# Moving work between queues and engines in the S5 stage of a two-layer hybrid trunk

## The chip, the cores and the metric

The kernel runs on one core of one Trainium2 chip. The metric is the device time of one execution in microseconds (us); lower is better. Engines are named as the profile names them: PE (TensorE matmul), PEld (TensorE weight load), DVE (VectorE), ACT (ScalarE), POOL (GpSimd) and SP (SyncE, which only issues transfers). Each of them works through its own program in order.

## The reference

One inference step of a trunk with two layers, for 1024 prompt tokens and 32 sample tokens that share all weights. Layer 0 mixes tokens by retention and forgetting attention, layer 1 by an S5 state-space layer with a gated linear unit. Each mixer is followed by cross-attention to 256 memory tokens and a squared-ReLU MLP. All of it is float32 with a model width of 1024. The change lies in the S5 mixer alone:

```
u = (h @ w_in_c).reshape(B, T, 64 groups, 16 channels)
bu = einsum(b_bar, u)                  # per group: 64 complex states
x_t = a * x_{t-1} + bu_t               # diagonal complex recurrence (associative scan over t)
y = Re(einsum(c, x)) + d * u
g = y @ w_glu;  out = g[..., :1024] * sigmoid(g[..., 1024:])
outputs also: the last state of the prompt and of the sample (real, imaginary)
```

## The kernel before, in words

Activations lie feature-major (features on partitions, tokens along the free axis) in three token groups of 384, 384 and 256 + 32. Each large product runs as three passes over exact splits x = hi + lo and w = hi + lo. A weight block is loaded by `wload` (L135, SP queue, two buffers `wst`), split by ACT (`wh`, L139) and DVE (`wl`, L140), and used by 72 matmuls.

The S5 layer works on chunks of 8 tokens, 132 chunks in all (128 of the prompt, 4 of the sample), in eight blocks f of 8 groups (128 features). For each block:

- `gemm` with `winc` gives u block by block; `evac_u` (L1438, DVE) moves each token group from PSUM to the tile `u`, scaled by the reciprocal rms.
- `s5_block` stores `u` to DRAM (`ud`, L1445) and loads it again in eight pieces (L1448) as the tile `U`, with one token of the chunk and one channel to a partition, so that one product contracts a whole chunk. `u` has two buffers and `U` three. It also loads the tables `Gm` (L1450) and `ET` (L1453); `Hm` (L1422) and `Tm` (L1424) of the next block are loaded after `outputs`.
- `states` multiplies `Gm` with `U` (PE), ACT copies the result into `VC` (L1467, L1468), and a rotation by the phase table `ET` turns the complex recurrence into a real one: p1 = VC * cos (L1471) and p2 = VC * sin (L1472), a sum and a difference (L1473, L1474), a scan for each part with the radii `RT` (L1479), and a second rotation back (L1482, L1483). Four instructions (L1488, L1489, twice each) put the states into `Xp`. Three small copies (L1491 to L1493) save the last states in `so` and put the sample's first state `x0s` into a column of `Xp`. `s5_radii` (L1429) fills `RT` for the next block.
- `outputs` multiplies `Tm` with `U` and `Hm` with `Xp`, ACT copies to `yt` (L1504), and the ACT queue stores it to `yd` (L1505).

After the eight blocks come the memory keys and values of layer 1 (`memory_k` and `memory_v`: `mt`, `wxk`, `wxv`), between whose products the last blocks' `states` and `outputs` are placed, then the loads of `yd` as `yf` (L1533), their splits (L1524, L1525) and the product with `wglu`.

The program of PE is written down in order. The object `po` counts the columns of the products laid out so far; `states` of a block is due S1 = 16.5 such microseconds after its `u` is complete and at least 12 after the `states` before it, `outputs` S2 = 20 after `states`. The programs of the other engines, and of the queues that they issue, are put in order by the framework's scheduler from priorities and its own model of time.

Of the kernel before, what the change touches and what calls it, by code (L numbers as in the profile page):

```python
"""Hybrid retention / forgetting-attention / S5 streaming step on one core.

Activations are feature-major: features on partitions, tokens along the free axis; the 1024 prompt
tokens and the 32 sample tokens share every weight (token groups of 384, 384 and 256 + 32).
Large float32 products run as three float32r passes over exact splits x = hi + lo, w = hi + lo
(hi*hi + hi*lo + lo*hi); small products run in float32.
"""
# [11 lines left out]
AF = mybir.ActivationFunctionType  # L19
# [12 lines left out]
class _Order:  # L32
    """The tensor engine's program is laid out piece by piece; a piece that waits for other engines
    is put off until enough other products stand before it."""
# [29 lines left out]
def _body(tc, A):  # L64
    nc = tc.nc
# [20 lines left out]
    with es:  # L86
# [17 lines left out]
        # ---------------- constants  # L104
# [22 lines left out]
        # ---------------- helpers  # L127
# [20 lines left out]
        # evacuations can be held back until the pool they write to may be opened  # L148
# [14 lines left out]
        def gemm(blocks, load, rhs, evac, gran, done=None, post=None, lead=0, final=(0, 1, 2)):  # L163
            """blocks of 128 outputs, gran at a time for each token group; the first `lead` advance together"""
            blocks = list(blocks)
            at = 0
            while at < len(blocks):
                n = gran(at) if callable(gran) else gran
                bl = blocks[at : at + n]
                at += n  # L170
                ws = [load(b) for b in bl]
                for g in final if at >= len(blocks) else range(3):
                    i = 0
                    while i < len(bl):
                        w = lead if lead else 1
                        lead = 0
                        pss = [bank()[:, : NG[g]] for _ in range(w)]
                        for k in range(8):
                            s = slice(k * 128, k * 128 + 128)
                            x = rhs(g, k)  # L180
                            for j in range(w):
                                wh, wl = ws[i + j]
                                mm3(pss[j], wh[:, s], wl[:, s], x[0], x[1], k == 0, k == 7)
                            po.tick()
                        for j in range(w):
                            def ev(b=bl[i + j], g=g, ps=pss[j]):
                                with tc.high_priority(offset=HP):
                                    evac(b, g, ps)
                                if post is not None:
                                    post(b, g)  # L190
                            submit(ev)
                        i += w
                    if done is not None and at >= len(blocks):
                        submit(lambda g=g: done(g), False)
# [9 lines left out]
        def rstd_cols(acc, nt, scale, half=False, r=None, tag="rc", ps=None):  # L204
            """acc: [128, nt*128] partial sums of squares by partition -> [128, nt] reciprocal rms.
            With r, the columns summed up still lack a factor r^2."""
            ps = bc() if ps is None else ps
            for t in range(nt):
                mm(ps[:, t : t + 1], acc[:, t * 128 : t * 128 + 128], ones_c, start=True, stop=True)
            ms = npl.tile([128, 4], F32, tag="ms", bufs=4, name="ms")  # L210
            if r is None:
                nc.vector.tensor_scalar(ms[:, :nt], ps[:, :nt], scale, EPS, op0=MULT, op1=ADD)
            else:
                r2 = npl.tile([128, 4], F32, tag="r2", bufs=3, name="r2")
                gtt(r2[:, :nt], r[:, :nt], r[:, :nt], op=MULT)
                stt(ms[:, :nt], ps[:, :nt], scale, r2[:, :nt], op0=MULT, op1=MULT)
                vtt(ms[:, :nt], ms[:, :nt], r2[:, :nt], op=MULT)
                nc.vector.tensor_scalar(ms[:, :nt], ms[:, :nt], EPS, None, op0=ADD)
            rc = npl.tile([128, 4], F32, tag=tag, bufs=4 if tag == "rc" else 6, name=tag)
            tails.append(gtt(rc[:, :nt], ms[:, :nt], mhalf[:, :nt], op=ALU.pow))  # L220
            if r is not None:
                gtt(rc[:, :nt], rc[:, :nt], r2[:, :nt], op=MULT)
            if half:
                nc.vector.tensor_scalar(rc[:, :nt], rc[:, :nt], 0.5, None, op0=MULT)
            return rc
# [21 lines left out]
        def update(o, g, ys, acc, gpost, xres, xout, last=False, row=False, scale=1.0 / 1024, half=False, r=None):  # L247
            """x + rmsnorm(y) * g; o gets the split of the new x times the next norm's gain, and its
            reciprocal rms by token, in columns or along a row of all partitions"""
# [71 lines left out]
        # ---------------- memory keys and values of a layer (prompt)  # L321
# [63 lines left out]
        # ---------------- state-space layer: discretisation and per-group chunk matrices  # L385
# [8 lines left out]
        def s5_prepare(sp):  # L394
# [10 lines left out]
            # angles lambda_im*dt * (1, 8, 16, ..., 512), reduced to [-pi, pi]  # L405
# [20 lines left out]
            # powers a^0..a^8  # L426
# [19 lines left out]
            # input gains  # L446
# [26 lines left out]
            def group(f):  # L473
# [20 lines left out]
                def cmul(xr, xi, pr, pi, n, nm, neg):  # L494
                    """outer products over (power, channel): real part and (negated) imaginary part"""
# [20 lines left out]
                # phase table e^{i n theta}, n = 1..128 and again 1..4  # L516
# [45 lines left out]
        # the tensor engine runs in the order written down  # L562
        es.enter_context(tc.manual_schedule(engines={mybir.EngineType.PE}))

        # ---------------- layer 0: input
# [41 lines left out]
        with tc.tile_pool(name="m0", bufs=1, reuse_waits="tile") as m0, tc.tile_pool(name="s5p", bufs=1, reuse_waits="tile") as s5p:  # L607
            # values and gates of the forgetting attention
# [43 lines left out]
            # log forget gates and their running sums  # L652
# [52 lines left out]
            # queries and keys of the forgetting attention  # L705
# [10 lines left out]
        # ---------------- layer 0: retention  # L716
# [29 lines left out]
        def chain(h, qT, kT, sil, step):  # L746
            """Chunks of queries/keys against themselves and the state before them, one after the other."""
# [23 lines left out]
            def values(t, p, kw, qs):  # L771
# [16 lines left out]
                # group norm over the head, back to feature-major, gate  # L788
# [56 lines left out]
        # ---------------- layer 0: forgetting attention  # L845
# [7 lines left out]
        with tc.tile_pool(name="m2", bufs=1, reuse_waits="tile") as m2:  # L853
            # causal masks, added to the scores by a product with the identity
# [7 lines left out]
            for s in range(2):  # L862
# [5 lines left out]
                # values beside ones: the last row of the product is the sum of the weights  # L868
# [22 lines left out]
            def fox_max(hd):  # L891
                """row maxima of the scores, negated, as two more rows of the query side; in pieces"""
# [32 lines left out]
            def fox_out(hd, more):  # L925
                """transposed scores, weights, values; more: the pieces of the next head's maxima"""
# [19 lines left out]
                def weigh(lo, hi, ri):  # L946
                    """the products over the sums, split"""
# [71 lines left out]
        # sample queries against the cache and themselves  # L1019
# [86 lines left out]
        def proj_out(nblk, load, rhs, evac_y, gpost, xres, xout, gran=4, lead=0, **kw):  # L1106
            """the product with the output weights, its norm and the residual; returns what becomes of it by group"""
# [35 lines left out]
        def close_after(stack, out, gs, then):  # L1143
            """before the first evacuation into it opens the next pool, where what comes before leaves off"""
# [7 lines left out]
        def cross(l, X, left, right):  # L1152
            """attention to the memory; returns its output and the pools to close behind it"""
# [11 lines left out]
            def parts(hd, name):  # L1165
                """two halves of an operand: of even heads in the pool, of odd heads in idle tiles of the norms"""
# [42 lines left out]
            def attend(hd, g):  # L1209
                """pieces of the attention of a head for a group of tokens, spread over the products that follow"""  # L1210
# [161 lines left out]
        def cross_mlp(l, X, p, last, left, right):  # L1372
            """returns the new x by group and the pools still in use"""
# [25 lines left out]
        # ---------------- layer 1: state-space mixer  # L1399
# [27 lines left out]
        def s5_radii(f):  # L1427
            RT = sd["RT"] = sd["sp"].tile([128, 4, 132], F32, tag="RT", bufs=1, name="RT")
            nc.vector.tensor_copy(RT, r8[:, 4 * f : 4 * f + 4][:, :, None].to_broadcast([128, 4, 132]))  # L1429
# [11 lines left out]
        def s5_block(f, u):  # L1441
# [3 lines left out]
            dma(Ud[f][:, :, :], u)  # L1445
            U = sd["su"].tile([128, 8, 132], F32, tag="U", bufs=3, name="U")
            for j in range(8):
                dma(U[16 * j : 16 * j + 16], Ud[f][:, j, :].rearrange("(g c) n -> c g n", c=16))  # L1448
# [6 lines left out]
            def states():  # L1455
                """chunk inputs to the states, and the states by a scan over the chunks"""
# [15 lines left out]
                gtt(p2, VC, sinb, op=MULT)  # L1472
# [10 lines left out]
                gtt(p2, p1, sinb, op=MULT)  # L1483
# [7 lines left out]
                nc.vector.tensor_copy(so[:, 8 * f : 8 * f + 8, 0], xg[:, :, 128])  # L1491
                nc.vector.tensor_copy(so[:, 8 * f : 8 * f + 8, 1], xg[:, :, 132])
                nc.vector.tensor_copy(xg[:, :, 128], x0s[:, 8 * f : 8 * f + 8])  # L1493
# [53 lines left out]
        gate = {}  # L1547
# [16 lines left out]
# ---------------------------------------------------------------- host side: layout only  # L1564
# [129 lines left out]
```

## Time and profile before

| | before |
|---|---|
| median of 3 runs | 3298.36 us (3295.52 to 3303.45) |
| span of the profiled execution | 3296.3 us |
| PE busy | 3160.3 us (96%) |
| DVE busy | 1495.2 us (45%) |
| ACT busy | 1071.6 us (33%) |
| POOL busy | 914.5 us (28%) |
| mean granted TensorE clock | 0.980 |

The only time that goes with the profiled execution is its span from the first to the last instruction, 3296.3 us. The median of the three runs is 2.1 us longer, and their lowest is 0.8 us shorter than that span. A busy share is a mean over stages with different limits; the stage that the change touches lies between about 1850 and 2056 us of the span. The granted clock is given as a share of 2.4 GHz, so that 0.50 is 1.2 GHz. Where an idle time is given with a releaser, that is the event that came last before the instruction began.

### The profile page before, as it was taken

How to read it: one execution, taken by the hardware profiler on the slowest of the kernel's cores; microseconds unless marked ns; L12 is line 12 of the kernel's file. 1: busy time of each engine (PE TensorE's matmuls, PEld its weight loads, DVE VectorE, ACT ScalarE, POOL GpSimd, SP SyncE). 2: the span in 40 equal slices, each digit the busy share in tenths (PEclk: the TensorE clock that was granted, in tenths of full speed). 3: DMA queues.
4: the chain of work that ended last, by engine and by line, in shares of the span. 5: the costliest groups of instructions: out<-in, count | busy, mean ns of one | idle time of the engine just before them, and what ended most of it. 6: DMA issues, size and time to landing. Idle time of an engine off the chain costs nothing.

```text
span 3296.3 us, 50246 instructions
## 1 busy us (share of the span) xinstructions
PE 3160.3 (96%) x19972; PEld 3059.2 (93%) x19972; DVE 1495.2 (45%) x2756; ACT 1071.6 (33%) x2117; POOL 914.5 (28%) x1182
## 2 busy tenths in 40 slices
PE   7999999998999999999999888998999999999997
PEld 7899986688999999999999878998999999999997
DVE  8843566527435223332334797227426132233224
ACT  5212335425435322221124334225435321222212
POOL 4873431216115211111114442015106111111115
PEclk9999999999999999999999998999999999999998
DMA  5562244124114211110112677114124110111113
GB/s 157 156 194 70 62 137 128 38 58 141 52 42 128 65 42 52 52 47 31 52 52 74 204 241 222 57 52 141 49 66 124 52 47 32 52 52 52 39 58 99
DMA packets 176336, 285.71 MB, mean 87 GB/s; under 512 B 34027, under 2 KB 130508, under 8 KB 175972
## 3 DMA queue, kind: packets, MB, share of 16 engines
q1 hardware_dynamic: 132310, 215.02, 21.8%
q10 hardware_dynamic: 35328, 41.83, 3.8%
q0 software_dynamic: 8464, 25.66, 2.3%
q8 instruction: 157, 2.57, 0.3%
q14 instruction: 77, 0.63, 0.1%
HBM read 220.17 MB, written 66.39 MB: 87 GB/s over the span
## 4 chain that ended last, share of the span: by engine, by line
PE 77%; DVE 7%; POOL 6%; DMA 4%; issue 4%; ACT 2%; SPq 0%; DVEq 0%; ACTq 0%; POOLq 0%
PE mm L72 68%; PE a L72 4%; PE b L72 2%; POOL q L527 2%; POOL acc L245 2%; PE c L72 1%; DVE xl L202 1%; DVE wl L140 1%; DVE upd L274 1%; POOL ET L528 1%; DMA ed<-ET 1%; POOL ET L529 1%; DVE upd L273 1%; PE b L76 1%; DMA mt<-in_memt_dram 0%
## 5 line engine op out<-in xcount | busy, mean ns | idle before, releaser
L72 PE MATMUL mm<-xh,wh 128*128 128x384 f32 (+1 forms) x3168 | 1050.4, 332 | 6.5 <-ACT mo L382 3.7
L72 PE MATMUL mm<-xh,wl 128*128 128x384 f32 (+1 forms) x3168 | 1031.4, 326 | 7.4 <-DVE wl L140 7.3
L72 PE MATMUL mm<-xl,wh 128*128 128x384 f32 (+1 forms) x3168 | 1031.9, 326 | 1.2 <-DVE xl L202 1.2
L72 PE MATMUL mm<-ho,wh 128*128 128x384 f32 (+1 forms) x3456 | 822.9, 324 | 1.5 <-DVE y L1366 1.5
L72 PEld LDWEIGHTS mm<-xh,wh 128*128 128x128 f32 x3168 | 603.5, 190 | 13.8 <-issue 5.0
L72 PEld LDWEIGHTS mm<-xh,wl 128*128 128x128 f32 x3168 | 602.4, 190 | 9.0 <-DVE wl L140 9.0
L72 PEld LDWEIGHTS mm<-xl,wh 128*128 128x128 f32 x3168 | 603.5, 190 | 1.8 <-DVE xl L202 1.8
L72 PEld LDWEIGHTS mm<-ho,wh 128*128 128x128 f32 x3456 | 603.5, 188 | 1.8 <-DVE y L1366 1.8
L72 PE MATMUL mm<-ho,wl 128*128 128x384 f32 (+1 forms) x1728 | 558.2, 323 | 0.0
L1347 POOL TENSOR_TENSOR ho<-u,ho 128x384 fp32r<-128x384 f32 (+1 forms) x192 | 183.3, 955 | 1176.2 <-ACT ho L1346 1150.4
L140 DVE TENSOR_TENSOR wl<-wst,wh 128x1024 fp32r<-128x1024 f32 (+1 forms) x252 | 318.5, 1264 | 416.0 <-ACT wh L139 412.8
L139 ACT ACTIVATE wh<-wst 128x1024 fp32r<-128x1024 f32 (+1 forms) x252 | 266.5, 1059 | 708.9 <-PE mm L72 641.6
L245 POOL TENSOR_TENSOR acc<-acc,sq 128x384 f32<-128x384 f32 (+2 forms) x259 | 280.9, 1093 | 412.1 <-ACT sq L244 406.5
L1366 DVE TENSOR_TENSOR y<-y,mm 128x384 f32<-128x384 f32 (+1 forms) x336 | 174.3, 519 | 353.4 <-PE mm L72 353.2
L72 PEld LDWEIGHTS mm<-ho,wl 128*128 128x128 f32 x1728 | 325.5, 188 | 0.0
L1344 DVE TENSOR_TENSOR u<-u 128x384 f32<-128x384 f32 (+1 forms) x192 | 103.3, 538 | 409.7 <-ACT u L1343 409.7
L1343 ACT ACTIVATE u<-mm 128x384 f32<-128x384 f32 (+1 forms) x192 | 88.0, 458 | 313.8 <-PE mm L72 313.6
L1346 ACT ACTIVATE ho<-u 128x384 fp32r<-128x384 f32 (+1 forms) x192 | 95.7, 498 | 172.1 <-DVE u L1344 172.1
L1206 POOL TENSOR_SCALAR p<-p,mx 128x256 f32<-128x256 f32 (+1 forms) x72 | 36.7, 510 | 241.4 <-DVE mx L1205 138.8
L202 DVE SCALAR_TENSOR_TENSOR xl<-upd,gall,xh 128x384 fp32r<-128x384 f32 (+1 forms) x120 | 100.0, 834 | 5.1 <-ACT xh L201 4.8
L244 ACT ACTIVATE sq<-y 128x384 f32<-128x384 f32 (+1 forms) x126 | 61.9, 495 | 109.7 <-DVE y L1366 56.2
L72 PE MATMUL mm<-xo,wh 128*128 128x384 f32 (+1 forms) x384 | 92.1, 324 | 0.0
(427 smaller groups left out, 4132.9 us busy)
## 6 DMA issues: line engine op xcount, KB each, us to landing
wst<-in_wup_dram SPq DMA_DIRECT2D x64, 512.0 KB
wst<-in_wdn_dram SPq DMA_DIRECT2D x64, 512.0 KB
xs<-upd ACTq DMA_DIRECT2D x80, 192.0 KB
xr<-xs SPq DMA_DIRECT2D x80, 192.0 KB
wst<-in_wab_dram SPq DMA_DIRECT2D x20, 512.0 KB
wst<-in_wxk_dram SPq DMA_DIRECT2D x16, 512.0 KB
wst<-in_wxv_dram SPq DMA_DIRECT2D x16, 512.0 KB
wst<-in_wxq_dram SPq DMA_DIRECT2D x16, 512.0 KB
```

The costliest lines, as they stand in the source:

```text
L72: return nc.tensor.matmul(out, lhsT, rhs, **kw)
L139: act(wh[:, :n], st[:, :n], AF.Copy)
L140: vtt(wl[:, :n], st[:, :n], wh[:, :n].bitcast(F32), op=SUB)
L202: stt(l, src, gain, h.bitcast(F32), op0=MULT, op1=SUB)
L244: act(sq[:, :n], src, AF.Square)
L245: return gtt(acc[:, :n], acc[:, :n], sq[:, :n], op=ADD)
L527: gtt(o[:, :, :, :m], ET[:, :, :, :m], a_, op=MULT)
L1343: act(t, ps, AF.Relu)
L1344: vtt(t, t, t, op=MULT)
L1346: act(h, t, AF.Copy)
L1347: gtt(lo, t, h.bitcast(F32), op=SUB)
L1366: vtt(Y[g][o], Y[g][o], ps, op=ADD)
```

## The change

Within the S5 stage, (1) the store of `u` and the eight loads of `U` of each block are issued by POOL and no longer by SP; (2) the product with the sines in both rotations is computed by DVE and no longer by POOL, so that DVE computes both products of both rotations; (3) the three small copies at the end of `states` and the copy that fills the radii are done by ACT and no longer by DVE. Line numbers stay as they are; comments and docstrings were removed as well.

```
 def s5_radii(f):
-    nc.vector.tensor_copy(RT, r8[:, 4 * f : 4 * f + 4][:, :, None].to_broadcast([128, 4, 132]))
+    act(RT, r8[:, 4 * f : 4 * f + 4][:, :, None].to_broadcast([128, 4, 132]), AF.Copy)
 ...
 def s5_block(f, u):
-    dma(Ud[f][:, :, :], u)
+    nc.gpsimd.dma_start(Ud[f][:, :, :], u)
     U = sd["su"].tile([128, 8, 132], F32, tag="U", bufs=3, name="U")
     for j in range(8):
-        dma(U[16 * j : 16 * j + 16], Ud[f][:, j, :].rearrange("(g c) n -> c g n", c=16))
+        nc.gpsimd.dma_start(U[16 * j : 16 * j + 16], Ud[f][:, j, :].rearrange("(g c) n -> c g n", c=16))
 ...
     def states():
         vtt(p1, VC, cosb, op=MULT)
-        gtt(p2, VC, sinb, op=MULT)
+        vtt(p2, VC, sinb, op=MULT)
 ...
         vtt(VC, p1, cosb, op=MULT)
-        gtt(p2, p1, sinb, op=MULT)
+        vtt(p2, p1, sinb, op=MULT)
 ...
-        nc.vector.tensor_copy(so[:, 8 * f : 8 * f + 8, 0], xg[:, :, 128])
-        nc.vector.tensor_copy(so[:, 8 * f : 8 * f + 8, 1], xg[:, :, 132])
-        nc.vector.tensor_copy(xg[:, :, 128], x0s[:, 8 * f : 8 * f + 8])
+        act(so[:, 8 * f : 8 * f + 8, 0], xg[:, :, 128], AF.Copy)
+        act(so[:, 8 * f : 8 * f + 8, 1], xg[:, :, 132], AF.Copy)
+        act(xg[:, :, 128], x0s[:, 8 * f : 8 * f + 8], AF.Copy)
```

## Rows read from the trace of the kernel before

**Rows 1.** Stretches: length, busy time by engine, granted clock, DMA share, GB/s.
```profile
1910.00:1980.00 70.00, 54.22 (x372) 52.90 (x372) 68.61 (x93) 26.66 (x61) 29.25 (x29) 0.95 0.77 253
1980.00:2000.00 20.00, 18.56 (x147) 18.39 (x147) 16.66 (x26) 3.62 (x7) 6.20 (x8) 0.92 0.73 220
2000.00:2056.00 56.00, 47.27 (x351) 45.21 (x350) 39.38 (x43) 32.66 (x51) 15.82 (x17) 0.90 0.72 226
```

**Rows 2.** Waits of PE, 1800 to 2060: releaser, total us, times, longest.
```profile
PE b L72 <- DMA Tm<-td: 7.1, 3, 2.9
PE mm L72 <- DVE u L1438: 5.7, 2, 4.4
PE a L72 <- DMA yd<-yt: 4.3, 1, 4.3
...
```

**Rows 3.** Timeline of POOL, block 4: start, duration, instruction, idle before.
```profile
1939.31 2.41 POOL L1472 TENSOR_TENSOR p<-VC,ET 128x1056 f32<-128x1056 f32 x1 [1.01 <-ACT xmh L201]
...
1947.88 2.64 POOL L1483 TENSOR_TENSOR p<-p,ET 128x1056 f32<-128x1056 f32 x1 [6.16 <-DVE ini L1476]
```

**Rows 4.** Timeline of DVE beside them, and one row of the tail.
```profile
1939.41 2.34 DVE L1493 COPY Xp<-x0s 128x8 f32<-128x8 f32 x1
1941.66 1.24 DVE L1471 TENSOR_TENSOR p<-VC,ET 128x1056 f32<-128x1056 f32 x1
...
1948.11 3.52 DVE L1482 TENSOR_TENSOR VC<-p,ET 128x1056 f32<-128x1056 f32 x1
...
2004.83 3.49 DVE L140 TENSOR_TENSOR wl<-wst,wh 128x1024 fp32r<-128x1024 f32 x1
```

**Rows 5.** Groups by line, shapes apart: count, busy us, mean ns, idle before.
```profile
L140 DVE TENSOR_TENSOR wl<-wst,wh 128x1024 fp32r<-128x1024 f32 x248 | 312.8, 1262 | 415.1 <-ACT wh L139 411.9 <-PE mm L72 3.0
L976 ACT ACTIVATE pT<-b 128x512 f32<-128x512 f32 x48 | 28.4, 593 | 32.3 <-PE b L72 32.2
L1472 POOL TENSOR_TENSOR p<-VC,ET 128x1056 f32<-128x1056 f32 x8 | 21.6, 2700 | 12.2 <-issue 6.8 <-ACT VC L1468 4.0 <-ACT xmh L201 1.4
L1482 DVE TENSOR_TENSOR VC<-p,ET 128x1056 f32<-128x1056 f32 x8 | 19.0, 2374 | 0.0
L1493 DVE COPY Xp<-x0s 128x8 f32<-128x8 f32 x8 | 11.5, 1432 | 0.0
L1471 DVE TENSOR_TENSOR p<-VC,ET 128x1056 f32<-128x1056 f32 x8 | 10.0, 1249 | 4.0 <-ACT VC L1468 4.0
```

**Rows 6.** Two lines' instructions: ns min/median/max, first and last start.
```profile
L1491 DVE COPY so<-Xp x8: 163/172/1966, 1889.1 to 2022.2; 128x8 f32<-128x8 f32 x8
...
L1429 DVE COPY RT<-r x8: 435/1303/2637, 1847.1 to 1984.9; 128x528 f32<-128x528 f32 x8
```

**Rows 7.** Transfers issued: ns min/median/max, first and last start; then landing of L1533 on POOL.
```profile
L1448 SPq DMA_DIRECT2D U<-ud x64: 303/429/1655, 1860.8 to 1986.1; - x64
L1424 POOL DMA_DIRECT2D Tm<-td x8: 530/530/602, 1847.7 to 2007.2; - x8
L1533 POOL DMA_DIRECT2D yf<-yd x4: 590/612/642, 2044.2 to 2046.0; - x4
DMA to landing us min/median/max: 4.8/5.1/5.2
```

**Rows 8.** Timeline of SP and PE around block 6's loads.
```profile
1952.32 0.34 SPq L1445 DMA_DIRECT2D ud<-u  x1
...
1965.37 0.30 SPq L1448 DMA_DIRECT2D U<-ud  x1
...
1968.74 0.69 PE L72 MATMUL a<-U,Gm 128*128 128x132 f32 x4 [4.28 <-DMA yd<-yt]
```

**Rows 9.** Timeline of POOL and PE around two table loads.
```profile
1846.87 0.81 POOL L1422 DMA_DIRECT2D Hm<-hd  x1
...
1936.68 0.53 POOL L1424 DMA_DIRECT2D Tm<-td  x1
...
1941.61 0.46 PE L72 MATMUL b<-U,Tm 128*128 128x132 f32 x2 [2.84 <-DMA Tm<-td]
```

## The prediction

> **What bounds the kernel now.** The page first: PE is busy for 96% of the span, so over the whole kernel only idle PE time, or a better granted clock, can be won. Then the table of stretches shows where such time lies in the stage that the change touches [rows 1]. Between 1910 and 1980 us PE works for 54.22 of 70 us and idles for 15.8, while DVE is busy for 68.61: there DVE is the bound, though over the span it is busy for only 45%. From 1980 to 2000 PE idles for 1.4 us, from 2000 to 2056 for 8.7. The granted clock is 0.95, 0.92 and 0.90 in these stretches; one minus the clock, times the busy time, is 2.7, 1.5 and 4.7 us, an estimate of what the lower level (1.2 GHz instead of 2.4) cost. Idle time and clock together are 34.8 us, about 1% of the time; no change in this stage can win more in it.
>
> Then the waits of PE [rows 2]. Three of them have to do with the change: `Tm` comes late three times (7.1 us), the copy of `u` out of PSUM comes late on DVE (5.7 us), and one wait of 4.3 us stands in front of the product of `Gm` and `U`. That last one is put down to the store of `yt`, but the timeline says otherwise: `u` of block 6 was stored at 1952.32, the last piece of `U` was issued at 1965.37, and the product began at 1968.74 [rows 8]. I read it as a wait for `U`. `Tm` is late because POOL issues it late: in block 4 it was issued at 1936.68 and PE began at 1941.61, 4.9 us later [rows 9], and POOL's program has the rotation's second product ahead of it, as at 1947.88 [rows 3].
>
> Last, the two timelines side by side. POOL's product runs from 1939.31 for 2.41 us; DVE's copy of eight columns into `Xp` (L1493) starts at 1939.41 and lasts 2.34 us, and the cosine product begins only then [rows 3, 4]. In the second rotation POOL works from 1947.88 for 2.64 us, and DVE's product L1482 lasts 3.52 us from 1948.11. The same shape alone takes 1.25 us (L1471), and the small copies next to L1493 take 0.17 (median) [rows 5, 6]. So DVE stands still for most of the time in which POOL computes: giving the product to POOL does not take it off DVE.
>
> The Trainium skill says so too (SBUF — State Buffer, section "SBUF: two separate sides"): DVE and GpSimd share one pair of ports as an exclusive lock held for a whole instruction. The trace agrees: 3.52 us against 1.25.
>
> **The change, part by part.**
>
> **The products (POOL to DVE).** Added to DVE: two products a block of the shape of L1471, 2 x 1.25 = 2.50 us. Removed from DVE a block, by means and medians [rows 5, 6]: `RT` 1.30, the column of `x0s` 1.43, the two `so` copies about 0.5 (median 0.17 each, one of them 1.97), and the stretch of L1482, 2.37 - 1.25 = 1.12. That is 4.35 us, net -1.85. Within the saturated stretch the pattern of rows 4 is commoner than the mean: 2.34 for the column, 2.27 of stretch, 0.34 for `so`, and an `RT` of 0.44, its shortest; 5.39 in all, net -2.9. I take -2.4 us a block between these two. Four blocks pass in the 70 us (a block every 17 us or so), so DVE's work there shrinks by 10 us (7 to 12). It stays the bound or nearly: PE has 54.2 us of work against the 58.6 left to DVE. So the 10 us come out of PE's idle 15.8, and the waits for `u` and most of those for `Tm` with them.
>
> **The clock.** If 10 of 15.8 us of idle time go, part of the 2.7 + 1.5 us lost at the lower clock comes back; I take 2 (0 to 4.2).
>
> **The tail, 2000 to 2056.** Block 7's rotations lie between the weight splits there. One `wl` took 3.49 us instead of 1.26 while POOL computed [rows 4, 5]; that and block 7's own 1.9 would give 4.1 us of DVE. But PE waits there mostly for weights that pass through two `wst` buffers one after the other, so I count 2 us (0 to 4.1).
>
> **The copies and radii (DVE to ACT).** ACT gets four instructions a block. `RT` is 528 columns; the nearest ACT row has 512 and takes 0.59 us. The copies of eight columns lie between DVE's 0.16 and that 0.59. So 1.1 to 2.4 us a block, on an engine that is busy for 26.66 of 70 us [rows 1, 5, 6]: the work itself is covered by ACT's idle time. The price is the order: `RT` waits for the scan, the copies for `Xp`, and behind them on ACT stand the evacuations of `VC` and `yt`, which free PSUM for PE, and the weight splits `wh`. The path from `Xp` to PE's `outputs` hardly changes: three short ACT copies replace 0.34 + 1.43 us on DVE. I take +1 us in all; from 0 to +1 a block, 8 in all.
>
> **The loads and stores of u (SP to POOL).** POOL loses 16 products, 8 x (2.41 + 2.64) = 40 us by the two durations in rows 3, and gets 64 pieces and 8 stores. The piece most like them is `yf` as POOL issues it, 0.61 us; a store is like `Tm`, 0.53 [rows 7]. So 39 + 4 = 43 us: its busy time stays. Eight pieces take 4.9 us instead of 8 x 0.43 = 3.4 on SP, so `U` is complete 1.5 us later where nothing else holds it. The chain is store 0.53, landing 5.1, pieces 4.9, landing 5.1: 15.6 us, taking the `yf` landing for both. `states` is due 16.5 us of products after `u` is complete, so this just fits; before, block 6 needed 1968.74 - 1952.32 = 16.4. In front of the waiting store and pieces on POOL stand `Gm`, `ET`, and behind them `Tm`, `Hm` and the small memset of `Xp`; PE waits for all of these. I take +1 us; from -4.3 (the wait before block 6's product goes, since `U` no longer stands behind other loads on SP) to +1.5 a block, 12 in all. SP loses 72 issues, and weight loads no longer stand behind stores that wait for `u`; PE hardly waits for weights in the saturated stretch, so I count nothing (at best the 2 us of the tail once more).
>
> A rule of the skill speaks against this part: while DVE runs an instruction that uses both ports, such as a float32 copy, GpSimd can't write its descriptors, and a transfer issued from its queue stalls (SBUF — State Buffer, the box on DVE blocking DMA in "SBUF: two separate sides"; it gives 620 ns becoming about 3100). One row bears it out weakly: `Hm` took 0.81 us to issue, `Tm` 0.53 in the median and at most 0.60, mostly with DVE saturated beside it [rows 7, 9]. It is part of the second rival.
>
> **Sum.** -10 (DVE) - 2 (clock) - 2 (tail) + 1 (ACT) + 1 (POOL) = -12. The profiled span of 3296.3 becomes 3284.3. The median of the runs is 2.1 us above that span, which I keep: 3286.4, given as 3286.
>
> **The rivals.**
>
> *All of PE's gaps close.* If DVE falls below PE in every block and SP, free of waits for `u`, runs weights and `U` ahead, then 15.8 + 1.4 + about 4 us of idle time and 6 of the 8.9 us of clock come back: 27 us, 3271. For it: DVE's 58.6 is near PE's 54.2. Against it: PE needs `U`, `Tm` and the rotations in turn, and the tail is paced by its loads. Chance 0.15.
>
> *POOL becomes the late one, and the kernel slower.* Place: POOL's program between two `outputs`. If a block's store and pieces are put ahead of the next `Tm`, then `Tm` is issued 0.53 + 5.1 + 4.9 = 10.5 us after its buffer comes free, or later if `u` is not ready, and lands 4.9 later: 15.4 us. PE has some 13.5 us until it needs it (54.2 / 4 for all its work in a block), less some 3 that `outputs` itself takes (16 products, an estimate from four of that width in 0.69 us [rows 8]): about 10.5. So PE would wait 5 us in each of six blocks, 30 us, where it now waits 18 in all; with the clock's share this is about 10 us over before, 3308. It decides from about 7 us between the release of `Tm` and its issue; at 5 it costs what it costs today. Issues stretched as the one `Hm` was (0.28 us x 72 = 20 us) push the same way. For it: POOL works in order, and a store that waits for `u` holds all behind it. Against it: `Tm` is issued at high priority, and it becomes ready with the pieces, not after them. Chance 0.20.
>
> *Nothing moves.* The transfers are the bound behind DVE: the DMA share is 0.77 in the saturated stretch and 0.72 in the tail [rows 1], and the same bytes must pass; the relief of DVE turns into waits for `Tm` and `U`, or is given back before the first product with `wglu`. Then about 3297. That the scheduler orders the added work so that DVE is no freer belongs here. Against it: 0.77 is not full. Chance 0.20.
>
> **How the numbers follow.** My forecast, 3276 to 3292, has 0.45, the others 0.15, 0.20 and 0.20. I call no change what lies within 0.2%, 6.6 us, which is about what a measurement of this kernel can tell: 3291.8 to 3305.0. Faster: 0.45 + 0.15, less 0.02 for the forecast's upper edge, 0.58. The case without movement and the edges of the others give 0.22 for the same, and 0.20 is slower. The range of 3268 to 3306 takes in the unmoved case and reaches halfway into the outer two, leaving out about 0.15.
>
> **What would show it.** Right: no POOL product in the stage; DVE's two products at 1.25 us each and L1482 never above 1.3; a stretch from block 2's to block 6's `states` that is some 10 us shorter, with the waits for `u` and `Tm` smaller; ACT's copies at 0.2 to 0.6 us. Wrong: waits of PE for `Tm` or `U` that have grown, with POOL idle before a store of `u` or a piece of `U` and `Tm` issued more than 7 us after `outputs`; or ACT idle before `RT` with `VC` behind it; or a stage that is shorter at 1980 and not at 2056.

## The result, and the profile after

The changed kernel is slower: 3322.39 us (median of 4 runs, 3321.72 to 3326.85) against 3297.13 for the kernel before (4 runs, 3295.52 to 3303.45), a ratio of 1.0073 with a 95% interval of 1.0059 to 1.0087: some 24 us more, where 12 less were forecast. The profiled execution spans 3321.2 us, 24.9 more than before.

First the table of stretches, with the columns of [rows 1].

```profile
1910.00:1980.00 70.00, 46.88 (x309) 46.55 (x309) 42.68 (x60) 22.57 (x59) 23.65 (x48) 0.80 0.61 190
1980.00:2000.00 20.00, 15.42 (x108) 15.02 (x106) 16.39 (x26) 8.89 (x23) 4.00 (x9) 0.98 0.68 189
2000.00:2056.00 56.00, 41.56 (x309) 40.75 (x310) 41.18 (x52) 22.12 (x40) 13.20 (x27) 0.87 0.72 219
```

DVE, 68.61 us busy before, is busy for 42.68: it is no longer the bound. Yet PE also does less, 46.88 instead of 54.22, at a lower granted clock (0.80 instead of 0.95), and the DMA share has fallen from 0.77 to 0.61. So no engine and no transfer rate limits this stretch: everything waits in turn. For what, the waits of PE tell (1800 to 2060, columns of [rows 2]).

```profile
PE a L72 <- DMA ud<-u: 12.1, 1, 12.1
PE a L72 <- DMA U<-ud: 11.0, 1, 11.0
PE b L72 <- ACT VC L1468: 7.5, 1, 7.5
PE a L72 <- ACT so L1491: 7.2, 1, 7.2
PE mm L72 <- DVE u L1438: 5.9, 1, 5.9
```

`Tm`, late three times before, is gone from the list. Three single waits, 12.1, 11.0 and 7.2 us, are new. The timeline of PE shows that all three stand before the first product of `Gm` with `U`, in blocks 2, 3 and 5, though each is put down to another releaser (rows between them left out).

```profile
1907.01 0.78 PE L72 MATMUL a<-U,Gm 128*128 128x132 f32 x2 [7.23 <-ACT so L1491]
...
1932.60 0.56 PE L72 MATMUL a<-U,Gm 128*128 128x132 f32 x1 [10.99 <-DMA U<-ud]
...
1974.78 0.56 PE L72 MATMUL a<-U,Gm 128*128 128x132 f32 x1 [12.12 <-DMA ud<-u]
```

The copy of `so` on ACT has nothing to do with that product; the cause is found on POOL, which issues `U`. Its timeline from block 2 on (start, duration, instruction, idle time before):

```profile
1887.55 0.53 POOL L1450 DMA_DIRECT2D Gm<-gd  x1 [0.73 <-PE b L72]
1888.38 3.18 POOL L1448 DMA_DIRECT2D U<-ud  x6 [0.30 <-issue]
1899.86 0.57 POOL L1424 DMA_DIRECT2D Tm<-td  x1 [8.30 <-PE a L72]
1900.41 0.13 POOL L1485 MEMSET Xp<- 128x8 f32 x1
1900.49 0.55 POOL L1422 DMA_DIRECT2D Hm<-hd  x1
1901.04 1.10 POOL L1448 DMA_DIRECT2D U<-ud  x2
...
1921.68 0.57 POOL L1424 DMA_DIRECT2D Tm<-td  x1 [8.43 <-PE a L72]
1922.23 0.13 POOL L1485 MEMSET Xp<- 128x8 f32 x1
1922.32 0.55 POOL L1422 DMA_DIRECT2D Hm<-hd  x1
1922.86 0.56 POOL L1448 DMA_DIRECT2D U<-ud  x1
...
1962.87 0.11 POOL L1485 MEMSET Xp<- 128x8 f32 x1 [5.67 <-PE a L72]
1963.35 0.57 POOL L1424 DMA_DIRECT2D Tm<-td  x1 [0.37 <-issue]
1963.91 0.55 POOL L1422 DMA_DIRECT2D Hm<-hd  x1
1964.46 1.11 POOL L1448 DMA_DIRECT2D U<-ud  x2
```

Six of block 2's eight pieces go out from 1888.38. Then comes the load of `Tm` for the next block, whose only buffer PE's `outputs` of block 0 is still to release, and POOL stands still for 8.30 us. The last two pieces wait behind it and go at 1901.04, and PE starts the product at 1907.01. Block 3's last piece stands behind the next `Tm` (idle for 8.43), block 5's last two behind the memset of `Xp` (idle for 5.67), which waits for PE as well. So PE, POOL and the transfers form a ring: `outputs` releases `Tm`, `Tm` lets the last pieces go, and PE's next `states` needs them. The fourth long wait, 7.5 us for `VC`, lies in the tail and outside this ring: it stands before `outputs` of block 6 (2033.43) and ends with `VC` of block 7. On ACT that `VC` stands behind splits of `yf`, for which ACT had been idle for 8.72 us, and behind two weight splits. How much of the loss it makes is open.

Landing takes longer than the 5.1 us assumed for some of them. For `U` and for the store of `u`, the times from issue to landing (min/median/max) are, in this order:

```profile
DMA to landing us min/median/max: 2.5/4.6/9.1
...
DMA to landing us min/median/max: 3.2/6.8/10.9
```

From the end of the last issue to the product it takes 4.9 us in block 2 (1902.14 to 1907.01), but 9.2 in blocks 3 and 5, so in these two the landing is a good part of the wait.

What the change did on DVE came out as meant (ns min/median/max, first and last start; compare [rows 5 and 6]):

```profile
L1482 DVE TENSOR_TENSOR VC<-p,ET x8: 1242/1257/1261, 1883.5 to 2042.7; 128x1056 f32<-128x1056 f32 x8
...
L1429 ACT ACTIVATE RT<-r x8: 642/642/648, 1848.6 to 2007.9; 128x528 f32<-128x528 f32 x8
...
L1491 ACT ACTIVATE so<-Xp x8: 215/216/217, 1889.4 to 2050.9; 128x8 f32<-128x8 f32 x8
```

### The profile page after: what moved, and what is told of

Its sections match the earlier page's. It is cut to its first block, busy times and chain, and to the rows that moved or that the text cites. A ratio compares the mean times of both kernels' runs of the same rounds, so it can differ in the third digit from the quotient of the medians.

```text
span 3321.2 us, 50207 instructions
## 1 busy us (share of the span) xinstructions
PE 3165.4 (95%) x19972; PEld 3066.0 (92%) x19972; DVE 1478.6 (45%) x2740; ACT 1078.3 (32%) x2149; POOL 906.6 (27%) x1238
## 4 chain that ended last, share of the span: by engine, by line
PE 70%; DVE 4%; DMA 2%; POOL 2%; issue 2%; ACT 1%; SPq 0%; ACTq 0%; DVEq 0%; POOLq 0%
PE mm L72 63%; PE a L72 4%; PE b L72 2%; POOL acc L245 1%; PE c L72 1%; DVE upd L274 1%; DMA yf<-yd 1%; DVE xl L202 1%; DVE upd L273 1%; PE b L76 1%; DMA wst<-in_wxv_dram 0%; DVE wl L140 0%; DMA ud<-u 0%; POOL rc L220 0%; DMA U<-ud 0%
## 5 line engine op out<-in xcount | busy, mean ns | idle before, releaser
L72 PEld LDWEIGHTS mm<-xh,wh 128*128 128x128 f32 x3168 | 604.0, 191 | 12.3 <-issue 5.0
```

Source lines behind the costliest of these rows:

```text
L72: return nc.tensor.matmul(out, lhsT, rhs, **kw)
```

## The experiments

Each ratio is to the kernel before, run on the same chip, with its 95% interval; 0.001 is 3.3 us. Letters name the theories of one expectation only. Runs called "products" start from the kernel before, the others say from what.

**u back on SP** (from the changed kernel)

```
-            nc.gpsimd.dma_start(Ud[f][:, :, :], u)
+            dma(Ud[f][:, :, :], u)
 ...
-                nc.gpsimd.dma_start(U[16 * j : 16 * j + 16], ...)
+                dma(U[16 * j : 16 * j + 16], ...)
```

> The changed kernel with the store of u and the loads of U back on SP; the products on DVE and the copies and radii on ACT stay. Theory A (the loss comes from POOL's program, in which the last pieces of U stand behind transfers that wait for PE): the long waits of PE before the product of Gm and U (7.2, 11.0 and 12.1 us in the changed kernel) go, DVE is no longer full between 1910 and 1980 us, and the time is 3280 to 3292 us, below the kernel before at 3297. Rival B (the products on DVE or the copies on ACT cost at least half of the 25 us): 3308 us or more.

3296.9 us, 0.9994 (0.9985 to 1.0003). The queue costs some 25 us, as A says, but the time misses A's range of 3280 to 3292: what is left doesn't win the 12 us forecast, so a second loss is hidden in the result.

**u on POOL alone** (the kernel before, with its products still on POOL)

```
-            dma(Ud[f][:, :, :], u)
+            nc.gpsimd.dma_start(Ud[f][:, :, :], u)
 ...
-                dma(U[16 * j : 16 * j + 16], ...)
+                nc.gpsimd.dma_start(U[16 * j : 16 * j + 16], ...)
```

> The kernel before with one edit: the store of u and the eight loads of U issued by POOL. Theory A: this edit alone costs at least as much as the whole change, since POOL also still computes its two products a block: 3318 to 3340 us, with waits of PE of 5 us or more before the product of Gm and U. Rival B: this edit costs little, 3294 to 3303 us.

3358.84 us, 1.0180 (1.0163 to 1.0197): 59 us, more than A's upper end. A piece of `U` or a store now stands behind POOL's products too, which wait for DVE and ACT. In POOL's timeline a product of 3.54 us is the next thing ahead of three pieces:

```profile
1918.91 0.56 POOL L1448 DMA_DIRECT2D U<-ud  x1 [8.01 <-DMA ud<-u]
1922.25 3.54 POOL L1472 TENSOR_TENSOR p<-VC,ET 128x1056 f32<-128x1056 f32 x1 [2.78 <-ACT VC L1468]
1925.74 1.62 POOL L1448 DMA_DIRECT2D U<-ud  x3
```

**Pieces first** (from the changed kernel; lines behind are one further down)

```
+            with tc.high_priority(offset=1000):
                 for j in range(8):
                     nc.gpsimd.dma_start(U[...], ...)
```

> The changed kernel with one edit: the eight loads of U of a block get a higher priority, so that in POOL's program they stand together ahead of the next Tm instead of two or more of them behind it. The same work on the same queue. Theory A in its narrow form (the order in POOL's program is the cause): the waits before the product of Gm and U shrink below 3 us each and the time falls by at least 15 us, to 3307 us or less. Rival C (the cause is the queue itself: the store of u lands late, 6.8 us in the median and up to 10.9, because the tables lie ahead of it in the same queue, and the loads wait for it): no gain over 5 us, 3317 us or more. Rival D (Tm now comes late instead): the waits move to the products of Tm and U, and the time lies between.

3309.39 us, 1.0039 (1.0027 to 1.0051): 11 of the 24 us are back. Block 2's eight pieces now all stand ahead of `Tm`, and its `states` begins at 1900.39 instead of 1907.01. From POOL's timeline:

```profile
1886.66 3.69 POOL L1449 DMA_DIRECT2D U<-ud  x7 [0.30 <-issue]
1891.50 0.53 POOL L1449 DMA_DIRECT2D U<-ud  x1 [1.15 <-DMA Gm<-gd]
1898.28 0.11 POOL L1486 MEMSET Xp<- 128x8 f32 x1 [6.25 <-PE a L72]
1898.77 0.57 POOL L1424 DMA_DIRECT2D Tm<-td  x1 [0.37 <-issue]
```

The edit raises nothing but the priority of these loads, so the order is worth some 11 us. That is less than A's narrow form asked for (3307 or less, no wait over 3 us). What the other 13 are in this version is not settled by it: PE still waits 6.8 us for `U` once, and in the tail 5.5 for `VC`.

**Tables on SP** (from the changed kernel): the loads of `Hm`, `Tm`, `Gm` and `ET` leave POOL, `u` and `U` stay there.

```
-            nc.gpsimd.dma_start(Tm, t_dram[:, 8 * f : 8 * f + 8, :])
+            dma(Tm, t_dram[:, 8 * f : 8 * f + 8, :])
 ... (Hm, Gm and ET likewise)
```

> The changed kernel with the loads of Hm, Tm, Gm and ET issued by SP instead of POOL, so that POOL issues the store and loads of u and has only the memset of Xp that waits for PE. Theory A (what costs is that transfers which wait for PE's outputs share POOL's program with the loads of U): the waits before the product of Gm and U shrink, and the time falls to 3295 to 3310 us. Rival C (POOL's own issuing or landing of the u transfers is what is slow): 3317 us or more. Rival D (the weights on SP now stand behind tables that wait for PE): no better than 3317, but with waits of PE for weights in place of those for U.

3295.43 us, 0.9998 (0.9989 to 1.0008). The whole loss of the queue is gone though POOL still issues all 72 transfers of `u` and `U`. So it isn't POOL's time for an issue, nor its kind of queue, but what stands among them. Nor is it a long landing by itself: the pieces of `U` land later here than in the changed kernel (2.5/4.6/9.1 there), and no wait of PE for `U` is left.

```profile
DMA to landing us min/median/max: 2.5/6.9/9.4
```

**Only the loads of U on SP** (from the changed kernel)

```
-                nc.gpsimd.dma_start(U[16 * j : 16 * j + 16], ...)
+                dma(U[16 * j : 16 * j + 16], ...)
```

> The changed kernel with the loads of U back on SP and only the store of u on POOL. Theory A (the pieces of U behind waiting Tm and memset cost the 25 us): about 3297 to 3303, most of the loss gone. Theory D (the store of u behind Tm and memset costs as much): 3306 to 3318, with PE's waits before the product of Gm and U put down to the store of u.

3296.29 us, 0.9997 (0.9988 to 1.0006), the same as with both on SP. The store on POOL costs nothing that can be measured; the pieces of `U` cost the 25 us.

**Products only**

```
-                gtt(p2, VC, sinb, op=MULT)
+                vtt(p2, VC, sinb, op=MULT)
 ...
-                gtt(p2, p1, sinb, op=MULT)
+                vtt(p2, p1, sinb, op=MULT)
```

> The kernel before with one edit: the sine products of both rotations on DVE instead of POOL. The price of the part by itself: if DVE stood still beside POOL's products, as the trace of before was read, DVE's work in a block shrinks by the stretches (about 2.2 us a rotation) and grows by two products of 1.25 us, so that the time is 3288 to 3297 us. If the stretches were harmless and the products are added work on a full engine: 8 blocks times 2.5 us, 3305 us or more.

3286.98 us, 0.9964 (0.9951 to 0.9977): 12 us faster than before and, level with the next run, the fastest of all versions. In its table of stretches PE does 59.02 us of work where it did 54.22:

```profile
1910.00:1980.00 70.00, 59.02 (x431) 57.95 (x429) 67.17 (x111) 27.67 (x62) 10.06 (x24) 0.96 0.85 264
```

The same work, from the start of block 2's `states` to the start of block 6's, before and then here: DVE is busy for 60.40 us instead of 68.71, and is still the bound.

```profile
1898.67:1968.74 70.07, 57.33 (x399) 55.90 (x397) 68.71 (x92) 23.51 (x57) 30.05 (x29) 0.98 0.78 251
```
```profile
1895.89:1957.20 61.31, 55.33 (x398) 54.21 (x397) 60.40 (x98) 23.41 (x57) 8.52 (x20) 1.00 0.91 285
```

And its DVE timeline holds a surprise: the small copies, still on DVE, take 0.17 us, where the column of `x0s` took 2.34 [rows 4].

```profile
1931.42 0.17 DVE L1491 COPY so<-Xp 128x8 f32<-128x8 f32 x1
1931.51 0.17 DVE L1492 COPY so<-Xp 128x8 f32<-128x8 f32 x1
1931.63 0.17 DVE L1493 COPY Xp<-x0s 128x8 f32<-128x8 f32 x1
1931.71 1.26 DVE L1471 TENSOR_TENSOR p<-VC,ET 128x1056 f32<-128x1056 f32 x1
```

**Products, and the radii on ACT**

```
-            nc.vector.tensor_copy(RT, ...)
+            act(RT, ..., AF.Copy)
```

> The kernel before with the sine products on DVE (3287 by itself) and, of the ACT part, only the copy that fills the radii. Theory A: with all copies on ACT the gain of 12 us was lost because ACT works in order and its RT stands ahead of the four evacuations of yt while it waits some 7 us for the scan; PE then waits for a PSUM bank. So this kernel loses most of the gain: 3293 to 3300 us, with waits of PE for yt. Rival B (the small copies, which wait for Xp in the midst of the evacuations of VC, are what costs): 3284 to 3290 us.

3287.14 us, 0.9968 (0.9956 to 0.9979). That the radii's wait for the scan holds up ACT's evacuations (A) has fallen: PE does wait for `yt` four times, 2.8 us in all, but the time is that of products only.

**Products, and the small copies on ACT**

```
-                nc.vector.tensor_copy(so[:, 8 * f : 8 * f + 8, 0], xg[:, :, 128])
+                act(so[:, 8 * f : 8 * f + 8, 0], xg[:, :, 128], AF.Copy)
 ... (L1492 and L1493 likewise)
```

> The kernel before with the sine products on DVE and, of the ACT part, only the three small copies. Theory A (RT is what costs): 3284 to 3291 us. Rival B (the small copies cost): 3293 to 3300 us. If both lose about 5 us the two parts add.

3300.2 us, 1.0006 (0.9996 to 1.0015): the three copies of 0.2 us eat the products' whole gain, 0.0042 or 14 us. ACT's timeline shows how:

```profile
1918.82 0.22 ACT L1491 ACTIVATE so<-Xp 128x8 f32<-128x8 f32 x1 [7.78 <-DVE Xp L1489]
1918.94 0.20 ACT L1492 ACTIVATE so<-Xp 128x8 f32<-128x8 f32 x1
1919.17 0.38 ACT L1467 ACTIVATE VC<-b 64x264 f32<-64x264 f32 x1
...
1921.28 0.39 ACT L1468 ACTIVATE VC<-b 64x264 f32<-64x264 f32 x1
```

ACT has waited 7.78 us for `Xp`, with evacuations of the next block's `VC` behind it, whose products PE had begun at 1909.39. `VC` is complete at 1921.67, and only then can DVE's next rotation begin. DVE, which was the bound, now idles in front of L1471 eight times, 17.2 us in all; in the products-only run it is twice, 3.7 us. These are the two lists of DVE's waits, 1860 to 2040, this run's first:

```profile
DVE p L1471 <- ACT VC L1468: 17.2, 8, 3.6
```
```profile
DVE p L1471 <- ACT VC L1468: 3.7, 2, 3.3
```

The 13.5 us between the two are about the 14 us lost.

**The same copies written later**: as the run above, with the three lines at the head of `outputs` instead of the end of `states`.

```
             def outputs(xg):
+                act(so[...], xg[:, :, 128], AF.Copy)
+                act(so[...], xg[:, :, 132], AF.Copy)
+                act(xg[:, :, 128], x0s[...], AF.Copy)
                 Hm, Tm = tabs[f]
```

> The kernel before with both sine products on DVE and the three small copies on ACT, as in the run with a ratio of 1.0006, but with the copies written at the head of outputs instead of at the end of states. ACT's program then has them behind the VC evacuations of the next states in most blocks, right ahead of the yt copies. Theory A (the cost of 13 us is ACT standing idle for Xp ahead of VC): the idle of 8 to 10 us before L1491 goes from ahead of VC, DVE's p1 no longer waits 2 to 4 us for VC, and the time falls to 3275 to 3289, the products' gain or better. Theory B (the copies' cost is that outputs itself starts later, because ACT's copies of x0s into Xp come later than DVE's would): still 3296 to 3304, or more, with PE waiting for ACT x0s.

3294.31 us, 0.9989 (0.9980 to 0.9999): between the two expectations. The timelines of ACT and DVE explain why. In block 3 the copies follow the next `VC`, and DVE's product starts without a wait:

```profile
1914.39 0.39 ACT L1468 ACTIVATE VC<-b 64x264 f32<-64x264 f32 x1
1916.38 0.22 ACT L1494 ACTIVATE so<-Xp 128x8 f32<-128x8 f32 x1 [1.60 <-DVE Xp L1489]
```
```profile
1917.20 1.25 DVE L1471 TENSOR_TENSOR p<-VC,ET 128x1056 f32<-128x1056 f32 x1
1935.23 1.26 DVE L1471 TENSOR_TENSOR p<-VC,ET 128x1056 f32<-128x1056 f32 x1 [3.65 <-ACT VC L1468]
```

From the next block on the scheduler has put them ahead of `VC` again, and the wait is back (3.65 us). So where the order changed, the wait went, and with it 0.0017 of the 0.0042, two fifths of the cost. The rest fits the wait that is left, 12.3 us over the same stretch, 8.6 more than in products only, where the time is 0.0025 or 8 us longer:

```profile
DVE p L1471 <- ACT VC L1468: 12.3, 5, 3.6
```

**The same copies on POOL** (products on DVE, radii on ACT)

```
-                nc.vector.tensor_copy(so[:, 8 * f : 8 * f + 8, 0], xg[:, :, 128])
+                nc.gpsimd.tensor_copy(so[:, 8 * f : 8 * f + 8, 0], xg[:, :, 128])
 ... (L1492 and L1493 likewise)
```

> The kernel before with both sine products on DVE, the radii on ACT, and the three small copies on POOL, which has no products left. Theory A (small copies cost what waits behind them): behind them on POOL stand Gm and ET of a later block, which are needed late, so the copies cost little and DVE loses about 2 us a block: 3276 to 3288. Theory B (taking them off DVE delays outputs, wherever they go): 3294 to 3304. Theory C (POOL's small copies hold DVE as its products did): DVE's instructions beside them stretch, 3285 to 3292.

3289.65 us, 0.9973 (0.9963 to 0.9982): hardly a loss, so that taking the copies off DVE does no harm by itself (B falls). The time is just above A's range and inside C's, but DVE's products beside the copies aren't stretched (L1471 and L1482 take 1.26 us at most), so C isn't borne out. No gain over products only either: the copies cost DVE only 3 x 0.17 us a block by now.

**Products, and u on POOL** (small copies and radii stay on DVE)

```
-                gtt(p2, VC, sinb, op=MULT)
+                vtt(p2, VC, sinb, op=MULT)
 ...
-                dma(U[16 * j : 16 * j + 16], ...)
+                nc.gpsimd.dma_start(U[16 * j : 16 * j + 16], ...)
 ... (the second product and the store of u likewise)
```

> The kernel before with the sine products on DVE and the store of u and the loads of U on POOL; the copies and radii stay on DVE. It differs from the changed kernel (3322) by the ACT part alone, and from the products alone (3287) by the queue alone. Theory A: the queue costs about 25 us here too, and the ACT part that cost 10 us with u on SP is partly hidden behind the waits for U: 3308 to 3322 us. Rival B (the ACT copies are needed for the loss, because they delay what POOL waits for): 3300 us or less.

3321.8 us, 1.0074 (1.0059 to 1.0089), the same as with everything changed. From products only the queue costs 35 us, and the copies and radii on ACT add nothing to that. Where `U` is late, `VC` is late anyway; that this is the reason is argued, not shown.

**Tables on SP, and the small copies on DVE** (from the changed kernel; both edits as above)

> The changed kernel with the loads of Hm, Tm, Gm and ET on the SP queue and the three small copies back on DVE; u and U stay on POOL, products on DVE, radii on ACT. If the two losses (queue 25, small copies 13) are separate, both are gone and the products' gain is left: 3279 to 3290. If they are not separate (with the tables on SP the queue's loss was gone but the copies' may have been partly covered), 3291 to 3299.

3292.72 us, 0.9982 (0.9973 to 0.9992). It is 0.0016, 5 us, better than with the copies on ACT and doesn't reach products only: the two losses cannot simply be subtracted. What keeps 6 us here wasn't separated. PE's longest wait in it is 9.2 us for `yt`, in front of block 6's `states`: ACT is idle for 3.41 us until a piece of `yf` has landed, with an evacuation of `yt` behind it. That is order once more, but no run tests it.

## Why the prediction was wrong, step by step

**The products (-10 us): right.** Products only won 12 us, with the clock's 2 and the tail's 2 in it, which the runs don't separate. From block 2's to block 6's `states` it takes 1957.20 - 1895.89 = 61.3 us; before it was 1968.74 - 1898.67 = 70.1, so 8.8 less where 10 were said. DVE's work there shrinks by 8.3 us (7 to 12 were said). L1482 never exceeds 1.28 us, and PE's waits for `Tm` fall from 7.1 us to 2.1:

```profile
PE b L72 <- DMA Tm<-td: 2.1, 3, 1.7
```

One point in the working was put in the wrong place: the 1.43 us of the `x0s` column and the 1.30 of `RT` were booked as saved by their move to ACT. The copies fell to 0.17 and 0.43 us (medians) without being moved, because POOL's product no longer ran beside them. After that the move could win little.

What the Trainium skill says of the shared port held as an exclusive lock (SBUF — State Buffer, section "SBUF: two separate sides") fits this: a copy of 0.17 us stretched to 2.34, and back with POOL's product gone. The Trainium skill's warning in the same section, that a transfer issued from POOL stalls beside a float32 copy on DVE, was part of the second rival. In the changed kernel it doesn't show: the 64 issues of `U` took 528/531/567 ns and were cheaper than the 0.61 us assumed, but `RT`, the float32 copy of 128x528, is on ACT there. Where it stays on DVE, in the run with products and `u` on POOL, the one issue of `U` that began shortly before it took 0.80 us:

```profile
2008.02 0.80 POOL L1448 DMA_DIRECT2D U<-ud  x1 [5.13 <-DMA ud<-u]
```
```profile
2008.26 0.43 DVE L1429 COPY RT<-r 128x528 f32<-128x528 f32 x1
```

The 0.81 us of `Hm` before [rows 9] lies beside such a copy too (1847.1 [rows 6]); with `RT` on ACT the same issue takes 0.65. So the traces agree with the warning, but 0.27 us on one issue of `U` is far too little for the 25 us.

**The copies and radii (+1 us, at most 8): mis-sized.** The price was named correctly as one of order, with `VC` behind the copies, and then put at between nothing and 1 us a block. With the products on DVE and `u` on SP it is 14 us. The radii, named first, cost nothing; the small copies cost it all. The step "the path from `Xp` to `outputs` hardly changes" looked at what follows the copies and not at what the engine could have done while it waited: `Xp` comes late in a block, so a copy that waits for it leaves ACT idle, 7.78 us in the rows shown. `VC` came up to 3.6 us too late for DVE, waiting eight times, on the engine that was the bound.

**The loads and stores of u (+1 us, at most 12): the step that failed.** It measured 25 us from the changed kernel and 35 from products only. The chain of 15.6 us against a due time of 16.5 counted issue and landing and took every piece as issued when its data was there. It left out that the pieces are in one program with transfers that wait for PE. `Gm` and `ET` were put in front of the pieces there, and `Tm`, `Hm` and the memset behind them; the runs show the reverse for the last pieces, which wait behind `Tm` and the memset. Even the slack taken from the landing (5.1 us) was too small: 6.8 in the median and 10.9 at most for the store of `u`.

**The second rival** named the right place, POOL's program between two `outputs`, and the right sign. Its mechanism was the wrong way round (`Tm` late), and its price (10 us) too small. The point set against it, that `Tm` is issued at high priority, probably did the damage: priority puts an instruction forward in the program, and its wait then holds all behind it. No run lowered that priority; giving the pieces a high one as well won back 11 us. "What would show it" named waits of PE for `U` with POOL idle; of its two signs of POOL being late, the first was seen and the second, a late `Tm`, was not: in the three rows shown `Tm` goes within 0.7 us of its release (for the first, PE's last product of `outputs` ends near 1899.8 and `Tm` starts at 1899.86). ACT idle ahead of `VC`, the other sign, was seen too, before the small copies and not before `RT`.

**That all gaps close, or nothing moves:** the first didn't come near. The second described the run with `u` back on SP by its time (0.9994) and not by its mechanism: there a gain of 12 and a loss of about the same size cancel.

**The sum** by the single runs is -12 (products) + 0 (radii) + 14 (small copies) + 25 (queue) = +27, against +24 measured. That it comes out so near is partly chance, since products, copies and queue overlap: -12 + 35 + 0, by the other order of adding them, is +23.

## What to carry to other kernels

Before a transfer or a small copy is moved to an engine with time to spare, write down that engine's program around the new place, and for each instruction ahead what it waits for: in-order issue makes every wait ahead yours, and busy shares don't show it. A load that a coming product needs should not share a queue with refills that wait for earlier products of the same engine, or it must be put ahead of them. When an operation is slow because of a neighbour, remove the neighbour first and look again, since the operation may no longer be worth moving.

## What the runs showed of the hardware that was not expected

A copy of 128x8 takes 0.17 us on DVE, 0.20 to 0.22 on ACT and 0.19 to 0.29 on POOL (medians of the three lines; at most 1.28 on POOL). An issue on POOL takes 0.53 us for a piece of `U`, at most 0.57 in the changed kernel, where SP takes 0.43 in the median and up to 1.66 [rows 7]. A transfer of `U` issued on POOL landed after 2.5 to 9.1 us in the changed kernel, 4.6 in the median, and after 2.5 to 7.7, 3.9 in the median, with the pieces put first.
